# TensorE in emission order through a two-layer hybrid attention trunk

## The chip, the cores and the metric

The kernel runs on one core of a Trainium2 chip. The time is that of one execution on the device in microseconds (us). The profile comes from one execution that the hardware profiler recorded. Instructions are dispatched from one program per engine: TensorE (PE) does matmuls and transposes, VectorE (DVE) and ScalarE (ACT) elementwise work, GpSimd (POOL) little here, SyncE (SP) issues most transfers.

## The reference

Two layers of d_model 1024 over a sequence of 1024, float32. Each layer normalises its input, projects it once, and feeds two attention mixers whose outputs are gated, projected, merged and added to the residual:

```python
def hybrid_layer(x, c, ...):                       # cut to its steps
    h = rms_norm(x, norm_g) * (1 + scale(c)) + shift(c)
    parts = split(h @ w_in, IN_SIZES)              # all projections in one weight
    a = stick_breaking_attention(q, k, v)          # 8 heads of 64, blocks of 128 queries
    b = native_sparse_attention(q, kc, vc, ks, vs, kw, vw, gate_logits)
    a, b = a * silu(z_a), b * silu(z_b)
    y = sigmoid(m_a) * (a @ w_proj_a) + sigmoid(m_b) * (b @ w_proj_b)
    return x + gate(c) * (y @ w_out)

def stick_breaking_attention(q, k, v):             # per block of queries
    z = q @ k.T * scale
    between = reverse_cumsum(log_keep) - log_keep  # log_keep = log_sigmoid(-z), below the diagonal
    w = exp(log_sigmoid(z) + between)
    return w @ v
```

The sparse attention (NSA) has a branch over compressed keys, one over the eight best blocks of 64 keys, and one over a sliding window of 256.

## The kernel before

A layer goes through six parts: the norm (`norm_first` for layer 0; `norm_half`, called in the `output` of the layer before, for layer 1), `early` (the projections that NSA needs, compressed keys and values), `nsa`, `sb` (stick-breaking attention), what is left of the fill, and `output`.

**Projections.** Every operand is held as a high and a low float32r part, and a projection is three matmuls per chunk of 128 channels: L194 (high by high), L196 and L198 (high by low, low by high), in `mm3_gen`. A tile `proj` is 128x512 or 128x256, with eight chunks, so 24 matmuls.

**Fill.** `queue_projections` puts the stick-breaking projections (q, k, v) and then eight groups of gate projections (`t_group("m", ...)`) as generators into a list, `self.fill`. `run_jobs` goes through the attention jobs of `nsa` and `sb`: it merges the scores' steps of one job with the weights-times-values steps of the job before, emits one step, and calls `pump` with a share of the job's estimated us; `pump` emits projection matmuls from the list until that much is used up. `drain_fill` emits what is left. `tick` and `defer` emit vector steps when an estimated clock has come far enough, `flush` all of them at once.

**Order.** What the code emits goes to the tile framework's scheduler, which sets each engine's order and the semaphores. It puts instructions that it takes to be ready ahead of ones that wait. Code inside `tc.manual_schedule(engines={...})` keeps the emission's order on the engines named. Before, `norm_first` alone is inside one, for PE, DVE and ACT.

**Names in the rows.** `sc` are scores in PSUM (L996 compressed ones, L872, L873 the others, with L875 for the mask; `kk` stacked keys, `q` queries, `KCS` compressed keys). `E` and `C` are ScalarE's results from them (L1245, L1246 for stick-breaking), which VectorE finishes (L1249 the reversed product scan, L1250; L1115 in NSA). `tr` L885 are transposes of E, `wh` and `wl` their split parts (L137), `av` L904, L905 the products with V. `x` L430 is the scaled input of the second layer's norm, `tr` L436 its transposes, `acthi` and `actlo` the normalised input in two parts. `raw` and `w` are weights as loaded and as split. q and kk come by DMA from the DRAM tensor `QK`, where `early` and the fill put them.

Of the kernel before, what the change touches and what calls it, by code (L numbers as in the profile page):

```python
# [10 lines left out]
F32 = mybir.dt.float32  # L11
# [10 lines left out]
S = 1024  # L22
D = 1024
# [64 lines left out]
class Trunk:  # L88
# [214 lines left out]
    def run(self):  # L303
        tc, nc, I = self.tc, self.nc, self.I
        with tc.tile_pool(name="const", bufs=1) as cp, \
                tc.tile_pool(name="big", bufs=1) as self.big, \
                tc.tile_pool(name="wpool", bufs=1) as self.wpool, \
                tc.tile_pool(name="stage", bufs=2) as self.stage, \
                tc.tile_pool(name="lay", bufs=1) as self.lay, \
                tc.tile_pool(name="dram", bufs=1, space=DRAM) as self.dram, \  # L310
                tc.tile_pool(name="pproj", bufs=1, space=PSUM) as self.pproj, \
                tc.tile_pool(name="psc", bufs=1, space=PSUM) as self.psc, \
                tc.tile_pool(name="ptr", bufs=1, space=PSUM) as self.ptr, \
                tc.tile_pool(name="pav", bufs=1, space=PSUM) as self.pav:
            self.consts = self.tl(cp, [P, NMASK - 2 * P], F32, "consts")
            self.ident = self.tl(cp, [P, P], F32, "ident")
            self.sc = self.tl(cp, [P, KD], F32, "silu_c")
            self.ones = self.tl(cp, [P, P], F32, "ones")
            nc.vector.memset(self.ones, 1.0)
            self.identb = self.tl(cp, [P, P], BF16, "identb")  # L320
            self.mask = {m: self.tl(cp, [P, P], BF16, m) for m in ("m_strict", "m_causal")}
            self.mods = {}
            for l in range(self.depth):
                self.plan_layer(l)
            xsrc = I["x"]
            with tc.manual_schedule(engines={mybir.EngineType.PE, mybir.EngineType.DVE, mybir.EngineType.Activation}):
                act = self.norm_first()
            for l in range(self.depth):
                dst = self.O["out"] if l == self.depth - 1 else self.tl(self.dram, [S, D], F32, f"x{l + 1}")
                act = self.layer(l, act, xsrc, dst)  # L330
                xsrc = dst


    def vectors(self, pool, l):
# [1124 lines left out]
```

## Time and profile before

| | |
|---|---|
| time, median of three runs (lowest, highest) | 2232.81 us (2227.79, 2235.55) |
| profiled execution, its own time | 2227.61 us |
| its span, first to last instruction | 2225.8 us |
| mean granted clock of TensorE | 0.990 |
| busy share PE, DVE, ACT, POOL | 95%, 71%, 51%, 3% |
| HBM read, written | 206.28 MB, 83.89 MB |

An engine's busy time is the time in which it has an instruction under way. Matmuls overlap, so the sum of their single times is greater than the busy time. In the granted clock 1.00 is the full clock, 2.4 GHz, and 0.50 the lower one, 1.2 GHz. The layers take about half the span each: NSA runs in layer 0 from about 293 to 682 us, stick-breaking from there to about 1000, and the same in layer 1 about 1080 us later.

### The profile page before, as it was taken

How to read it: one execution, taken by the hardware profiler on the slowest of the kernel's cores; microseconds unless marked ns; L12 is line 12 of the kernel's file. 1: busy time of each engine (PE TensorE's matmuls, PEld its weight loads, DVE VectorE, ACT ScalarE, POOL GpSimd, SP SyncE). 2: the span in 40 equal slices, each digit the busy share in tenths (PEclk: the TensorE clock that was granted, in tenths of full speed). 3: DMA queues.
4: the chain of work that ended last, by engine and by line, in shares of the span. 5: the costliest groups of instructions: out<-in, count | busy, mean ns of one | idle time of the engine just before them, and what ended most of it. 6: DMA issues, size and time to landing. Idle time of an engine off the chain costs nothing.

```text
span 2225.8 us, 36846 instructions
## 1 busy us (share of the span) xinstructions
PE 2124.4 (95%) x13128; PEld 1833.5 (82%) x13128; DVE 1573.0 (71%) x3722; ACT 1129.9 (51%) x2489; POOL 73.0 (3%) x242
## 2 busy tenths in 40 slices
PE   4999999999999999999999998999999999999999
PEld 3898778988887777779889986889898877777899
DVE  5768558868765877886766852887788487787643
ACT  4433147656565655663433421665666465656410
POOL 2200000000000000010011000000000000001000
PEclk8999999999999999999999999999999999999999
DMA  7545852253116445275555355222522364534443
GB/s 287 113 136 189 251 154 81 91 152 94 64 48 159 128 130 129 81 245 177 164 151 161 107 192 141 90 90 82 146 92 68 97 151 113 146 98 166 148 124 104
DMA packets 254104, 297.05 MB, mean 133 GB/s; under 512 B 38888, under 2 KB 201568, under 8 KB 253920
## 3 DMA queue, kind: packets, MB, share of 16 engines
q1 hardware_dynamic: 213152, 250.65, 37.4%
q10 hardware_dynamic: 36224, 29.37, 5.1%
q0 software_dynamic: 4544, 14.68, 2.3%
q8 instruction: 103, 1.69, 0.3%
q14 instruction: 81, 0.66, 0.1%
HBM read 206.28 MB, written 83.89 MB: 130 GB/s over the span
## 4 chain that ended last, share of the span: by engine, by line
PE 66%; DVE 18%; DMA 7%; issue 4%; ACT 3%; POOL 1%; SPq 0%; ACTq 0%; DVEq 0%; POOLq 0%
PE proj L194 15%; PE proj L198 15%; PE proj L196 15%; PE tr L885 5%; DVE C L1249 4%; PE av L905 4%; PE av L904 3%; PE sc L872 3%; PE sc L873 3%; DVE wl L137 3%; DMA ada<-in_ada_w 2%; DVE E L1250 2%; DVE w L137 2%; DMA q<-QK 1%; DMA actlo<-AD 1%
## 5 line engine op out<-in xcount | busy, mean ns | idle before, releaser
L194 PE MATMUL proj<-acthi,w 128*128 128x512 f32 x1312 | 537.6, 410 | 3.0 <-ACT acthi L136 2.2
L196 PE MATMUL proj<-actlo,w 128*128 128x512 f32 x1312 | 538.0, 410 | 0.0
L198 PE MATMUL proj<-acthi,w 128*128 128x512 f32 x1312 | 537.2, 409 | 0.0
L136 ACT CAST w<-raw 128x512 fp32r<-128x512 f32 (+1 forms) x296 | 183.3, 623 | 227.3 <-PE proj L198 129.7
L194 PEld LDWEIGHTS proj<-acthi,w 128*128 128x128 f32 x1312 | 250.2, 191 | 43.6 <-ACT acthi L136 2.7
L137 DVE TENSOR_TENSOR wl<-tr,wh 128x512 fp32r<-128x512 f32 (+2 forms) x432 | 257.0, 611 | 40.7 <-ACT wh L136 38.3
L196 PEld LDWEIGHTS proj<-actlo,w 128*128 128x128 f32 x1312 | 250.0, 191 | 38.1 <-DVE actlo L137 0.8
L198 PEld LDWEIGHTS proj<-acthi,w 128*128 128x128 f32 x1312 | 249.6, 190 | 37.1 <-DVE w L137 0.2
L137 DVE TENSOR_TENSOR w<-raw,w 128x512 fp32r<-128x512 f32 (+1 forms) x296 | 202.5, 689 | 81.9 <-ACT w L136 80.6
L136 ACT CAST wh<-tr 128x512 fp32r<-128x512 f32 (+2 forms) x432 | 221.3, 527 | 76.4 <-PE tr L885 71.3
L194 PE MATMUL proj<-w,acthi 128*128 128x256 f32 (+1 forms) x768 | 221.5, 289 | 5.4 <-DVE s L137 2.4
L905 PE MATMUL av<-wl,V 128*128 128x256 f32 (+1 forms) x864 | 217.6, 285 | 7.6 <-DVE wl L137 7.4
L198 PE MATMUL proj<-w,actlo 128*128 128x256 f32 (+1 forms) x768 | 221.1, 288 | 0.0
L196 PE MATMUL proj<-w,acthi 128*128 128x256 f32 (+1 forms) x768 | 220.0, 286 | 0.0
L904 PE MATMUL av<-wh,V 128*128 128x256 f32 (+1 forms) x864 | 216.7, 271 | 1.2 <-DVE o L923 0.5
L1249 DVE TENSOR_TENSOR_SCAN C<-C 128x128 f32<-128x128 f32 (+7 forms) x128 | 172.7, 1350 | 55.0 <-ACT C L1245 54.5
L885 PE MATMUL tr<-ident,E 128*128 128x128 f32 x1152 | 187.4, 276 | 24.2 <-DVE E L1250 23.4
L885 PEld LDWEIGHTS tr<-ident,E 128*128 128x128 f32 x1152 | 139.1, 140 | 68.1 <-DVE E L1250 35.4
L905 PEld LDWEIGHTS av<-wl,V 128*128 128x128 f32 x864 | 162.7, 188 | 31.0 <-DVE wl L137 19.7
L872 PE MATMUL sc<-kk,q 128*128 128x512 f32 (+3 forms) x512 | 176.8, 346 | 8.8 <-DVE mx L1085 4.1
L873 PE MATMUL sc<-kk,q 128*128 128x512 f32 (+3 forms) x512 | 175.5, 343 | 0.0
L904 PEld LDWEIGHTS av<-wh,V 128*128 128x128 f32 x864 | 163.0, 189 | 13.7 <-ACT wh L136 3.6
(247 smaller groups left out, 3902.8 us busy)
## 6 DMA issues: line engine op xcount, KB each, us to landing
raw<-in_w_in SPq DMA_DIRECT2D x168, 256.0 KB, 3.0
ada<-in_ada_w SPq DMA_DIRECT2D x48, 512.0 KB, 5.1
kk<-QK SPq DMA_DIRECT2D x48, 512.0 KB, 8.6
q<-QK ACTq DMA_DIRECT2D x64, 256.0 KB, 4.2
QK<-s SPq DMA_DIRECT2D x32, 512.0 KB, 3.0
MD<-sz SPq DMA_DIRECT2D x64, 256.0 KB, 2.5
QK<-s SPq DMA_DIRECT2D x48, 256.0 KB, 3.9
VD<-s SPq DMA_DIRECT2D x48, 256.0 KB, 2.0
```

The lines of the kernel that those rows point to most:

```text
L136: nc.scalar.copy(hi, src)
L137: nc.vector.tensor_tensor(lo, src, hi.bitcast(F32), ALU.subtract)
L194: nc.tensor.matmul(ps, lh, rh, start=(x == 0), stop=False)
L196: nc.tensor.matmul(ps, lh, rl, start=False, stop=False)
L198: nc.tensor.matmul(ps, ll, rh, start=False, stop=(x == n - 1))
L872: nc.tensor.matmul(ps, q, k[:, 0, c0:c1], start=True, stop=False)
L873: nc.tensor.matmul(ps, q, k[:, 1, c0:c1], start=False, stop=not masks)
L885: nc.tensor.transpose(pt[:, x * P:x * P + P], b, self.ident)
L904: nc.tensor.matmul(ps[:, c:d], lhsT, hi[:, a:b], start=(first and x == 0), stop=False, skip_group_check=True)
L905: nc.tensor.matmul(ps[:, c:d], lhsT, lo[:, a:b], start=False, stop=(last and x == n - 1), skip_group_check=True)
L1249: nc.vector.tensor_tensor_scan(rev, rev, rev, 1.0, ALU.mult, ALU.bypass)
L1250: nc.vector.tensor_tensor(e[:, 0:nk], e[:, 0:nk], c[:, 1:nk + 1], ALU.mult)
```

## The change

The whole loop over the layers, with `norm_first`, is put into `manual_schedule` for PE. `norm_first` keeps its own for DVE and ACT, nested in it. Each line from L333 on stands one line further down in the kernel after (L872 is L873 there).

```diff
-            with tc.manual_schedule(engines={mybir.EngineType.PE, mybir.EngineType.DVE, mybir.EngineType.Activation}):
-                act = self.norm_first()
-            for l in range(self.depth):
-                dst = self.O["out"] if l == self.depth - 1 else self.tl(self.dram, [S, D], F32, f"x{l + 1}")
-                act = self.layer(l, act, xsrc, dst)
-                xsrc = dst
+            with tc.manual_schedule(engines={mybir.EngineType.PE}):
+                with tc.manual_schedule(engines={mybir.EngineType.DVE, mybir.EngineType.Activation}):
+                    act = self.norm_first()
+                for l in range(self.depth):
+                    dst = self.O["out"] if l == self.depth - 1 else self.tl(self.dram, [S, D], F32, f"x{l + 1}")
+                    act = self.layer(l, act, xsrc, dst)
+                    xsrc = dst
```

Three places of TensorE's program follow, as they stand before and after. The numbers in a tile's name tell one tile from another; the last of them differ by two between the kernels.

The start of layer 0's NSA stage before: the first compressed scores (`sc_482`) stand behind a run of fill, of which two tiles' last rows are shown.

```order
L196 MATMUL proj_530_3169<-actlo1_29_138,w_460_2836 128x512
L198 MATMUL proj_530_3169<-acthi1_28_137,w_460_2836 128x512
L194 MATMUL proj_530_3169<-acthi1_28_137,w_462_2841 128x512
L196 MATMUL proj_530_3169<-actlo1_29_138,w_462_2841 128x512
L996 MATMUL sc_482_3010<-KCS_126_595,q_481_3007 128x16 x4
L996 MATMUL sc_497_3058<-KCS_126_595,q_481_3007 128x32 x4
L198 MATMUL proj_530_3169<-acthi1_28_137,w_462_2841 128x512
```

The scores of this and the next step, `sc_497`, stand together, in the middle of a fill tile. The same place after, where `proj_473` to `proj_476` are the modulation's and gate's products of `early`:

```order
L412 MATMUL proj_473_2967<-acc2_381_2339,ones_4_87 128x512
L412 MATMUL proj_474_2970<-acc2_381_2339,ones_4_87 128x512
L374 MATMUL proj_475_2973<-ones_4_87,acc1_387_2349 128x1 x8
L374 MATMUL proj_476_2984<-ones_4_87,acc0_388_2350 128x1 x8
L997 MATMUL sc_482_3012<-KCS_126_597,q_481_3009 128x16 x4
L194 MATMUL proj_496_3053<-acthi0_26_137,w_458_2833 128x512
L196 MATMUL proj_496_3053<-actlo0_27_138,w_458_2833 128x512
L198 MATMUL proj_496_3053<-acthi0_26_137,w_458_2833 128x512
```

The scores `sc_482` moved ahead of the first fill tile, `proj_496`, and of all that stood before them up to `proj_530`.

The start of layer 0's stick-breaking stage before:

```order
L194 MATMUL proj_1754_8268<-acthi0_26_135,w_1594_7555 128x512
L196 MATMUL proj_1754_8268<-actlo0_27_136,w_1594_7555 128x512
L872 MATMUL sc_1715_8101<-kk_1710_8090,q_1712_8095 128x128
L873 MATMUL sc_1715_8101<-kk_1710_8090,q_1712_8095 128x128
L875 LDWEIGHTS identb_5_89
L875 MATMUL sc_1715_8101<-m_strict_6_90,identb_5_89 128x128
L872 MATMUL sc_1718_8118<-kk_1710_8090,q_1712_8095 128x256
```

Here too the scores of two steps stand together inside a fill tile. The same place after:

```order
L194 MATMUL proj_1707_8046<-acthi0_26_137,w_1596_7562 128x512
L873 MATMUL sc_1715_8103<-kk_1710_8092,q_1712_8097 128x128
L874 MATMUL sc_1715_8103<-kk_1710_8092,q_1712_8097 128x128
L876 LDWEIGHTS identb_5_89
L876 MATMUL sc_1715_8103<-m_strict_6_90,identb_5_89 128x128
L196 MATMUL proj_1707_8046<-actlo0_27_138,w_1596_7562 128x512
L198 MATMUL proj_1707_8046<-acthi0_26_137,w_1596_7562 128x512
L194 MATMUL proj_1707_8046<-acthi0_26_137,w_1598_7567 128x512
L196 MATMUL proj_1707_8046<-actlo0_27_138,w_1598_7567 128x512
L198 MATMUL proj_1707_8046<-acthi0_26_137,w_1598_7567 128x512
L194 MATMUL proj_1707_8046<-acthi0_26_137,w_1598_7567 128x512
L873 MATMUL sc_1718_8120<-kk_1710_8092,q_1712_8097 128x256
```

The first stick-breaking scores, `sc_1715`, stand ahead of what is left of `proj_1707` and of the tiles after it up to `proj_1754`, and fill stands between them and the next scores, `sc_1718`.

The layer boundary before, where `proj_2759` and `proj_2761` are layer 1's first projections:

```order
L198 MATMUL proj_2759_13230<-acthi0_2550_12056,w_2702_12958 128x512
L194 MATMUL proj_2761_13268<-acthi0_2550_12056,w_2696_12943 128x512
L196 MATMUL proj_2761_13268<-actlo0_2551_12057,w_2696_12943 128x512
L198 MATMUL proj_2761_13268<-acthi0_2550_12056,w_2696_12943 128x512
L436 MATMUL tr_2725_13115<-ident_2_85,x4_2634_12508 128x128
L436 MATMUL tr_2727_13124<-ident_2_85,x4_2634_12508 128x128
L436 MATMUL tr_2729_13133<-ident_2_85,x4_2634_12508 128x128
L194 MATMUL proj_2761_13268<-acthi0_2550_12056,w_2696_12943 128x512
```

The transposes come one at a time, as x becomes ready, with projections between them. The same place after:

```order
L198 MATMUL proj_2713_13058<-w_2682_12816,yl0_2553_12061 128x256
L437 MATMUL tr_2725_13117<-ident_2_85,x4_2634_12510 128x128 x4
L437 MATMUL tr_2727_13126<-ident_2_85,x4_2634_12510 128x128 x4
L437 MATMUL tr_2729_13135<-ident_2_85,x4_2634_12510 128x128 x4
L437 MATMUL tr_2731_13144<-ident_2_85,x4_2634_12510 128x128 x4
L437 MATMUL tr_2733_13153<-ident_2_85,x4_2634_12510 128x128 x4
L437 MATMUL tr_2735_13162<-ident_2_85,x4_2634_12510 128x128 x4
L437 MATMUL tr_2737_13171<-ident_2_85,x4_2634_12510 128x128 x4
L437 MATMUL tr_2739_13180<-ident_2_85,x4_2634_12510 128x128 x4
L194 MATMUL proj_2759_13232<-acthi0_2550_12058,w_2696_12945 128x512
```

All 32 transposes of the norm's second half moved ahead of the first projection of layer 1; before, they were spread among these projections.

## Rows read from the trace of the kernel before

**Rows 1.** The page: span, and busy time, share and instructions of each engine.

```profile
span 2225.8 us, 36846 instructions
PE 2124.4 (95%) x13128; PEld 1833.5 (82%) x13128; DVE 1573.0 (71%) x3722; ACT 1129.9 (51%) x2489; POOL 73.0 (3%) x242
```

**Rows 2.** The page: the chain that ended last, share of the span by engine.

```profile
PE 66%; DVE 18%; DMA 7%; issue 4%; ACT 3%; POOL 1%; SPq 0%; ACTq 0%; DVEq 0%; POOLq 0%
```

**Rows 3.** Windows: length, busy (count) of PE, PEld, DVE, ACT, POOL, PEclk, DMA, GB/s.

```profile
210.00:260.00 50.00, 50.00 (x216) 40.38 (x216) 30.45 (x33) 11.16 (x19) 0.00 (x0) 1.00 0.85 267
700.00:740.00 40.00, 35.99 (x212) 27.65 (x211) 36.97 (x50) 29.28 (x67) 1.19 (x12) 1.00 0.44 119
800.00:900.00 100.00, 94.41 (x541) 76.24 (x540) 79.30 (x108) 59.85 (x136) 2.38 (x24) 1.00 0.49 130
```

**Rows 4.** Windows around the starts of NSA and stick-breaking in both layers.

```profile
292.80:303.80 11.00, 10.85 (x39) 8.36 (x40) 0.61 (x3) 1.28 (x1) 0.00 (x0) 0.82 1.08 236
682.30:692.40 10.10, 10.10 (x44) 7.89 (x42) 0.00 (x0) 0.59 (x1) 0.00 (x0) 1.00 1.06 260
692.40:694.80 2.40, 0.14 (x2) 0.11 (x1) 0.00 (x0) 1.28 (x1) 0.00 (x0) 1.00 1.14 266
696.00:699.40 3.40, 3.40 (x10) 2.62 (x9) 1.32 (x3) 0.74 (x2) 0.20 (x2) 0.50 1.06 216
1373.60:1382.60 9.00, 9.00 (x39) 6.92 (x37) 1.59 (x4) 1.28 (x1) 0.00 (x0) 1.00 1.07 287
1382.60:1389.10 6.50, 0.04 (x1) 0.00 (x0) 0.00 (x0) 0.00 (x0) 0.00 (x0) 0.72 1.10 244
1389.20:1395.70 6.50, 6.50 (x21) 5.53 (x21) 2.77 (x14) 1.20 (x4) 0.00 (x0) 0.50 0.51 110
1770.90:1780.90 10.00, 10.00 (x45) 8.08 (x43) 0.00 (x0) 1.87 (x2) 0.00 (x0) 1.00 1.07 269
```

**Rows 5.** The chain that ended last, from 285 us: start, us, what.

```profile
290.03 13.65 DMA q<-QK
```

**Rows 6.** Timeline of PE: start, us, instruction, [idle before, releaser].

```profile
407.87 0.55 PE L885 MATMUL tr<-ident,E 128*128 128x128 f32 x3
694.73 0.30 PE L872 MATMUL sc<-kk,q 128*128 128x128 f32 x1 [2.26 <-DMA kk<-QK]
700.04 0.35 PE L872 MATMUL sc<-kk,q 128*128 128x384 f32 x1
794.38 0.38 PE L905 MATMUL av<-wl,V 128*128 128x256 f32 x1 [0.31 <-DVE wl L137]
1148.38 0.52 PE L436 MATMUL tr<-ident,x 128*128 128x128 f32 x3 [0.19 <-DVE x L430]
1169.88 0.36 PE L194 MATMUL proj<-w,acthi 128*128 128x256 f32 x1 [1.42 <-DVE s L137]
```

**Rows 7.** Timeline of ACT and DVE at two of these places.

```profile
695.42 0.27 ACT L1246 ACTIVATE E<-sc 128x128 f32<-128x128 f32 x1
1147.48 2.84 DVE L430 TENSOR_SCALAR x<-x,nri 128x1024 f32<-128x1024 f32 x4
```

**Rows 8.** Windows of tile proj alone: length, PE, PEld, DVE, ACT, PEclk, DMA, GB/s.

```profile
63.80:83.20 19.40, 5.60 (x37) 5.08 (x37) 0.84 (x2) 0.73 (x2) 1.00 0.26 62
349.50:353.50 4.00, 3.29 (x12) 2.08 (x12) 0.00 (x0) 0.00 (x0) 1.00 0.43 131
354.50:359.50 5.00, 3.81 (x13) 2.28 (x13) 0.68 (x1) 0.12 (x1) 1.00 0.31 107
405.60:407.90 2.30, 1.81 (x13) 1.60 (x12) 0.42 (x1) 0.37 (x1) 1.00 0.17 66
596.90:599.60 2.70, 1.92 (x6) 1.07 (x6) 0.00 (x0) 0.31 (x1) 1.00 0.25 97
1141.70:1158.60 16.90, 14.89 (x57) 9.83 (x56) 1.67 (x4) 1.48 (x4) 1.00 0.63 139
```

**Rows 9.** Waits of PE: waiting and releasing group, us in total, times, longest us.

```profile
PE tr L885 <- DVE E L1250: 23.4, 38, 1.1
```

## The prediction

> **What bounds the kernel now.** I read the page's busy times first. TensorE's matmuls cover 2124.4 of 2225.8 us [rows 1], so 101.4 us of idle is all that there is. The chain that ended last runs 66% through TensorE, 18% through VectorE and 7% through transfers [rows 2]. TensorE therefore sets most of the time, and what makes it idle is added to the end, unless later idle time takes the delayed work back.
>
> Then I read the stages. In the dense stretch from 210 us 216 matmuls take all of 50 us, 0.23 us each [rows 3]: no room. In the stick-breaking stage the engine is busy 94.4 of 100 us against VectorE's 79.3, and in that stage's opening 40 us VectorE leads, 37.0 against 36.0 [rows 3]. Attention is a string of short waits, and fill projections stand in them. Who puts them there is the question: the emission (`pump`, by its own estimate in us) or the scheduler, which moves matmuls on top of that. In the order listings the two kernels have the same instructions, and most of TensorE's program reads alike in both. They part in clusters: the half-1 chunks of the first norm, the start of each NSA stage, the start of each stick-breaking stage, the layer boundary, and some two dozen small places. At each of them the order before has projections ahead of a waiting attention step or transpose, and the order after has them behind it.
>
> So the method is this. At each cluster I count the projections that ran before the waiting instruction and no longer can. If the waiting instruction becomes ready when it did before, TensorE now stands idle for that time, and the projections run later, in stages that have no room. The loss is then about their busy time.
>
> **The change part by part.** All sums are made against the profiled execution's own time, 2227.61 us; the median of the three runs, 2232.81, is 5.2 above it, and I add that at the end.
>
> *T1, the first norm.* From 63.8 to 83.2 us 37 projection matmuls of 5.6 us [rows 8] run between the waits of the norm's chunks on VectorE. In order they come behind. Bounds 0 (the same chunks may come a little sooner where no projection is in their way) and 5.6; I take 4.
>
> *T2, the start of the NSA stage, twice.* The first compressed scores need q, and the chain shows its transfer from 290.03 for 13.65 us, so until 303.68 [rows 5]. TensorE was busy 10.85 of the 11.0 us before it, with 39 instructions, all but one of them fill [rows 4]. The order after has the scores first: about 11 us of idle, at full clock 9.0 us of work put off (layer 1 has the same 39 in 9.0 us [rows 4]). A second place follows 46 us later, where twelve and thirteen projections, 3.29 and 3.81 us, stand in two waits of the scores and transposes for VectorE [rows 8]. The low end is the first place alone, 9; the high end both, 9.0 + 7.1 = 16. I take 13, since the second place's wait may shrink when VectorE's steps are fed sooner. Twice: 26.
>
> *T3, the start of the stick-breaking stage, twice.* The same pattern with kk: 10.1 us filled with 44 instructions, then 2.26 us of idle until the scores at 694.73 [rows 4, 6]. In order TensorE waits through all of it. Layer 1 has 45 in 10.0 us [rows 4]. Here something comes back. The order before also holds the third score matmul until 700.04 [rows 6], although ScalarE had emptied its buffer at 695.42 + 0.27 = 695.69 [rows 7]: 4.35 us that the emission's order doesn't have. So 10.1 - 4.35 = 6 at the low end; 11 at the high one, with nothing back and the small places after it; I take 8. Twice: 16.
>
> *T4, the layer boundary, once.* The 32 transposes of norm half 1 are emitted ahead of layer 1's first projections. They need x, which VectorE scales at 1147.48 for 2.84 us [rows 7], the first of them being ready at 1148.38 [rows 6], and they then go at the pace of the modulation. 57 projection matmuls, 14.89 us in a window of 16.9, filled this [rows 8]. In order they follow. A wait of 1.42 us at 1169.88 for the projections' own successors [rows 6] can vanish: 14.89 - 1.42 = 13.5, and as half 0's chunks have a small place of the same kind I take 14. Low end 9 (the wait for x ends sooner, nothing else does), high end 17, the whole window.
>
> *T5, seven smaller waits of each NSA stage.* In the first, thirteen projections (1.81 us) stand ahead of transposes that become ready at 407.87, when VectorE has scaled E; in the last, six (1.92 us) [rows 6, 8]. The seven add up to 15.4 us of projections. Bounds: half of it, 8, if a wait is partly the wait for steps that fill itself delayed; 17 with the smallest places that I left out. I take 14. Twice: 28.
>
> *T6, the stick-breaking stage's small waits.* About ten places per layer have three projections, 0.7 us, moved from ahead of a waiting step to behind it, as ahead of the av matmul at 794.38 that still waited 0.31 us [rows 6]. Before, these waits were not all covered either: 38 waits for E cost 23.4 us [rows 9]. Twenty times 0.7 is 14, if nothing comes back. The next uncovered wait can take some of it back, most of it at the low end, 4. I take 10, nearer to nothing coming back, since the waits for E come at every step.
>
> *T7, the granted clock.* After the idle 2.26 us ahead of 694.73 the row from 696.0 shows a granted clock of 0.50 for 3.4 us, and after the 6.5 us ahead of 1389.1 one of 0.50 for 6.5 us [rows 4]; that is the lower level, 1.2 GHz. Half a stretch is lost: 1.7 and 3.3 us. The change makes idle stretches of such lengths at four places that had none (layer 0's NSA start, both stick-breaking starts' longer ones, the boundary): 4 x 2.5 = 10. Low end 0, if no new stretch follows. The high end is the first rival.
>
> Nothing is added to any engine's work: the listings of the other engines change only near these places, GpSimd's not at all, and the number of instructions and transfers is the same. That the fill is taken later lets its weight loads go out later too, which I cost at nothing: SP's queue holds them ahead of need, and the q and kk transfers may land a little sooner for it, which lies within the low ends of T2 and T3.
>
> Sum: 4 + 26 + 16 + 14 + 28 + 10 + 10 = **108 us**. 2227.6 + 108 + 5.2 = **2341**.
>
> **The rivals.**
>
> *Clock.* If each of the 18 in-order stalls of T2, T3 and T5 is followed by a stretch at the lower level, not four places, T7 is 18 x 1.7 to 3.3, or 31 to 59 us. The other terms sum to 98: 2227.6 + 98 + 31 + 5.2 = 2362, up to 2390. For it: the two stretches named. Against it: fill projections follow each short wait at once, and the small waits of the trace before, up to 1.1 us for E [rows 9], leave a clock of 1.00 in the row from 800 us [rows 3]. The page "TensorE: Matmul & The Clock Gate" of the Trainium skill describes in its section "HAM oscillation — how this bites in real kernels" a kernel whose matmuls wait for a transfer at every tile and fall back to the low clock at every tile. By that account this rival would be the forecast, about 2376; the two rows with 0.50 agree with it, the row from 800 us doesn't for its shorter waits.
>
> *Smaller loss.* The short waits of T5 and T6 could cost nothing: the attention steps no longer stand behind fill, VectorE and ScalarE get their inputs sooner, so that the waits shrink and the later idle time takes the fill back. Then T1 to T4 remain, 4 + 26 + 16 + 14 = 60: 2227.6 + 60 + 5.2 = 2293. For it: those 23.4 us of waits for E [rows 9] are idle time that delayed fill can use. Against it: a wait that was covered by 13 projections [rows 8] is now bare. The page "Perfetto Trace Analysis" of the Trainium skill says, in "Identifying the Most-Contended Engine", that matmul busy time is a poor measure of how near a kernel is to its bound. If the 95% overstates, this rival gains; in the dense stretch the trace speaks against it, with 216 matmuls back to back.
>
> *Faster.* VectorE's chain, not TensorE, could be what ends the attention stages; then fill in front of scores and transposes delays the chain, and emission order lifts that. Its place is the stick-breaking start, its price 4.35 us (695.69 to 700.04 [rows 6, 7]), twice: 2232.8 - 8.7 = 2224. It decides if the work put off finds room: the 101.4 us of idle [rows 1] would take all of it. For it: VectorE leads in the first 40 us of that stage. Against it: it is 15 us behind in the 100 us from 800 [rows 3], and T4's stage has projections to do whichever way it goes.
>
> *No effect.* The moved projections fall into other waits one for one, or the scheduler's order and the emission's come to the same at run time because every queue waits anyway: 2232, give or take 7. The listings show 39 matmuls changing sides of one wait, so I give it little.
>
> **How the numbers follow.** The forecast has 0.60, clock 0.17, smaller loss 0.14, faster 0.05, no effect 0.04. About 0.3% is what a measurement of this kernel can tell from no change. Three cases are slower by more: 0.91; within it lies no effect, 0.04; faster 0.05. The ends of the terms add up to 0 + 18 + 12 + 9 + 16 + 4 + 0 = 59 and 5.6 + 32 + 22 + 17 + 34 + 14 + 59 = 184 us, which will not all meet on one side. The range from 2290 to 2385 keeps nearly all of the forecast, most of the clock rival and half of the smaller loss, and leaves out the rest, about 2 in 10.
>
> **What would show it.** In the profile after, TensorE's waits should list q at about 11 us per layer, kk at about 12 in layer 0 and 10 in layer 1, and x at the boundary at about 6 us or more; the busy total should stay within some 20 us of 2124 and the idle time grow by about 90. T7 shows as new stretches of 0.50 behind these waits, the clock rival as such stretches all through the NSA stage. Smaller loss shows if the waits in T5's places are short. The prediction is wrong if the stages between the clusters become shorter than they were: that is delayed fill finding room, and the step that fails then is that the loss equals the busy time moved.

## The result

The changed kernel takes 2333.47 us (median of four runs, 2331.44 to 2342.53) where the kernel before takes 2232.53 us beside it: a ratio of 1.0464, 95% interval 1.0435 to 1.0493, slower by about 101 to 104 us. The forecast was 2341, the range 2290 to 2385.

The profiled execution took 2331.58 us. Its page answers to [rows 1]:

```profile
span 2329.8 us, 36825 instructions
PE 2133.9 (92%) x13128; PEld 1846.2 (79%) x13128; DVE 1584.8 (68%) x3722; ACT 1136.5 (49%) x2489; POOL 72.4 (3%) x242
```

The span grew by 104.0 us. TensorE's busy time grew by 9.5 us with the same 13128 matmuls, so its idle time grew from 101.4 to 195.9, by 94.5. That is the form which the prediction gave: about 90 us of idle, and a busy time within 20 us of the old one. The next view says what the idle time waits for. It is the list of TensorE's waits (what waits, what released it, us in total, times, longest):

```profile
PE sc L997 <- DMA q<-QK: 28.4, 2, 15.1
PE sc L873 <- DMA kk<-QK: 27.9, 4, 12.3
PE tr L886 <- DVE E L1251: 24.6, 28, 1.6
PE tr L886 <- DVE E L1116: 21.6, 26, 1.7
PE av L906 <- DVE wl L137: 17.3, 24, 1.1
PE tr L437 <- DVE x L431: 9.0, 7, 6.5
PE sc L873 <- DVE mx L1086: 5.0, 6, 1.6
```

The waits for q and kk were 6.7 and 2.3 us; they are now 28.4 and 27.9. E from L1116 (L1115 before) stood with no row of note; now it has 26 waits of 21.6 us. The waits of stick-breaking for E [rows 9] hardly grew, 23.4 to 24.6 us. The one for x, 6.5 us, is at the layer boundary.

The timeline shows the long ones at their places (start, length, instruction, idle before it and its releaser):

```profile
306.21 0.99 PE L997 MATMUL sc<-KCS,q 128*128 128x16 f32 x4 [13.27 <-DMA q<-QK]
424.77 0.33 PE L886 MATMUL tr<-ident,E 128*128 128x128 f32 x1 [1.10 <-DVE E L1116]
727.04 0.45 PE L873 MATMUL sc<-kk,q 128*128 128x128 f32 x1 [11.42 <-DMA kk<-QK]
1194.65 1.05 PE L437 MATMUL tr<-ident,x 128*128 128x128 f32 x2 [6.47 <-DVE x L431]
1447.12 0.99 PE L997 MATMUL sc<-KCS,q 128*128 128x16 f32 x4 [15.09 <-DMA q<-QK]
1872.35 0.47 PE L873 MATMUL sc<-kk,q 128*128 128x128 f32 x1 [12.29 <-DMA kk<-QK]
```

And the windows behind these waits have the lower clock (from:to, length, busy and count of PE, PEld, DVE, ACT, POOL, granted clock, DMA, GB/s):

```profile
306.20:309.80 3.60, 3.59 (x11) 3.02 (x12) 1.51 (x9) 0.23 (x1) 0.00 (x0) 0.50 1.03 196
727.00:733.40 6.40, 6.36 (x18) 5.23 (x19) 1.83 (x4) 1.69 (x5) 0.20 (x2) 0.50 1.06 211
1195.00:1201.00 6.00, 5.20 (x20) 3.58 (x19) 5.21 (x8) 2.19 (x3) 0.00 (x0) 0.50 0.12 27
1447.10:1453.60 6.50, 6.48 (x19) 5.50 (x20) 3.01 (x17) 0.49 (x2) 0.00 (x0) 0.50 0.72 150
1872.40:1876.90 4.50, 4.50 (x14) 3.73 (x15) 0.77 (x3) 0.91 (x4) 0.10 (x1) 0.50 1.05 216
```

**Where the time came from.** The order of the two kernels meets again between the clusters. At such a point I take the start of the same instruction in both traces, and how much its delay grew since the point before. Idle is span less busy time of TensorE between the points; the clock's cost is half of the busy time that lies at half clock. All in us.

| stretch | from, to in the trace before | delay grew | idle grew | clock cost grew |
|---|---|---|---|---|
| first norm, early | 0 to 291.9 | 0.5 | 3.1 | -1.3 |
| NSA start, layer 0 | to 365.1 | 17.3 | 17.9 | -0.4 |
| rest of NSA, layer 0 | to 650.6 | 15.4 | 10.9 | 1.7 |
| stick-breaking start, layer 0 | to 726.8 | 8.2 | 7.9 | 1.5 |
| rest of it, layer 0 | to 1032.7 | 3.4 | 4.9 | 0.0 |
| norm half 0 | to 1075.4 | 2.1 | 1.8 | 0.0 |
| layer boundary | to 1169.9 | 11.9 | 7.7 | 4.5 |
| early, layer 1 | to 1302.5 | -0.8 | 0.1 | 0.0 |
| NSA start, layer 1 | to 1453.7 | 13.2 | 13.2 | 0.0 |
| rest of NSA, layer 1 | to 1739.2 | 17.8 | 11.9 | 3.4 |
| stick-breaking start, layer 1 | to 1811.3 | 12.3 | 11.0 | 2.3 |
| rest of it and output, layer 1 | to 2126.2 | 2.7 | 4.0 | 0.1 |

The rows sum to 104.0, 94.4 of idle and 11.8 of clock. They don't add up in each row, since matmuls that overlap less also count as busy, and ones that overlap more count as less.

### The profile page after: what moved, and what is told of

It reads as the page before. It is cut to its first block, busy times and chain, and to the rows that moved or that the text cites. A ratio compares the mean times of both kernels' runs of the same rounds, so it can differ in the third digit from the quotient of the medians.

```text
span 2329.8 us, 36825 instructions
## 1 busy us (share of the span) xinstructions
PE 2133.9 (92%) x13128; PEld 1846.2 (79%) x13128; DVE 1584.8 (68%) x3722; ACT 1136.5 (49%) x2489; POOL 72.4 (3%) x242
## 4 chain that ended last, share of the span: by engine, by line
PE 67%; DVE 18%; DMA 6%; ACT 3%; issue 3%; SPq 1%; POOL 1%; ACTq 0%; DVEq 0%; POOLq 0%
PE proj L196 16%; PE proj L194 15%; PE proj L198 15%; PE tr L886 5%; DVE C L1250 4%; PE av L906 4%; PE av L905 3%; PE sc L873 3%; PE sc L874 3%; DVE E L1251 2%; DMA kk<-QK 2%; DVE wl L137 2%; DVE w L137 2%; DMA q<-QK 1%; DMA actlo<-AD 1%
## 5 line engine op out<-in xcount | busy, mean ns | idle before, releaser
L137 DVE TENSOR_TENSOR wl<-tr,wh 128x512 fp32r<-128x512 f32 (+2 forms) x432 | 260.2, 612 | 65.1 <-ACT wh L136 62.7
L886 PE MATMUL tr<-ident,E 128*128 128x128 f32 x1152 | 191.2, 278 | 47.1 <-DVE E L1251 24.6
L906 PE MATMUL av<-wl,V 128*128 128x256 f32 (+1 forms) x864 | 217.5, 284 | 17.6 <-DVE wl L137 17.3
L873 PE MATMUL sc<-kk,q 128*128 128x512 f32 (+3 forms) x512 | 174.8, 341 | 36.8 <-DMA kk<-QK 27.9
```

Source lines behind the costliest of these rows:

```text
L137: nc.vector.tensor_tensor(lo, src, hi.bitcast(F32), ALU.subtract)
L873: nc.tensor.matmul(ps, q, k[:, 0, c0:c1], start=True, stop=False)
L886: nc.tensor.transpose(pt[:, x * P:x * P + P], b, self.ident)
L906: nc.tensor.matmul(ps[:, c:d], lhsT, lo[:, a:b], start=False, stop=(last and x == n - 1), skip_group_check=True)
```

## Experiments

Ratios are to the kernel before in runs beside it on the same chip, with their 95% intervals. A statement on one place rests on one trace of each kernel.

### One stage at a time

Three kernels set only a part in emission order; the scheduler keeps the rest. In the traces TensorE's order differs from the kernel before at that part's clusters alone.

```diff
-        self.nsa(l)
+        with self.tc.manual_schedule(engines={mybir.EngineType.PE}):
+            self.nsa(l)
```

> The kernel before with TensorE in emission order in the two NSA stages alone. In the changed kernel the delay over the kernel before grew there by 17.3 + 15.4 us in layer 0 and 13.2 + 17.8 us in layer 1, 63.7 in all. If the loss is made at each place by itself: 2232.5 + 64 = 2296, from 2291 to 2301, with waits for q of about 13 and 15 us. If later stages give part back when they have not lost time themselves (smaller loss): below 2285.

```diff
-        self.sb(l)
-        self.drain_fill()
+        with self.tc.manual_schedule(engines={mybir.EngineType.PE}):
+            self.sb(l)
+            self.drain_fill()
```

> The kernel before with TensorE in emission order in the two stick-breaking stages alone. The delay grew there by 8.2 + 3.4 us in layer 0 and 12.3 + 2.7 us in layer 1, 26.6 in all: 2259, from 2255 to 2263, if each place loses by itself. If VectorE's chain bounds the stage and gains from the lifted hold of the third score matmul (faster rival): 2224 to 2232.

```diff
+            with tc.manual_schedule(engines={mybir.EngineType.PE}):
                 act = self.output(0, xsrc, x1)
                 self.head(1, act)                  # early and queue_projections
+            # likewise norm_first with head(0), and output(1); nsa and sb outside
```

> TensorE in emission order in the first norm, both layers' early projections and the outputs with the layer boundary; the scheduler orders the NSA and stick-breaking stages. In the changed kernel the delay grew there by 0.5 + 2.1 + 11.9 = 14.5 us: ratio 1.0065, from 1.005 to 1.008, if each place loses by itself. With the runs of the NSA stages alone and the stick-breaking stages alone it should sum to the whole change's 1.046. If the loss at the boundary came from the attention stages' delays before it: under 1.003.

Measured: NSA alone 1.0257 (1.0240 to 1.0274), 57 us; stick-breaking alone 1.0124 (1.0106 to 1.0142), 27 us; norms and boundary alone 1.0070 (1.0052 to 1.0088), 16 us. Together 1.0451 against the whole change's 1.0464. The waits of the first two, stage by stage, have nearly the rows of the whole change in them. TensorE's waits with NSA alone in emission order:

```profile
PE sc L996 <- DMA q<-QK: 29.3, 2, 15.4
PE tr L885 <- DVE E L1250: 23.0, 38, 1.1
PE tr L885 <- DVE E L1115: 21.6, 26, 1.7
```

and with stick-breaking alone:

```profile
PE tr L885 <- DVE E L1250: 24.6, 28, 1.6
PE sc L872 <- DMA kk<-QK: 20.3, 2, 10.4
PE av L905 <- DVE wl L137: 14.0, 16, 1.1
```

With NSA alone, E in NSA has its 21.6 us and E in stick-breaking (38 times, 23.0) stays as before; with stick-breaking alone it is the other way round. So the loss is made at each place by itself, and next to nothing is paid back by a later stage: 3.0 us at the start of layer 0's stick-breaking with NSA alone, in its one trace. That is the premise of the sum, and it speaks against the rivals "smaller loss" and "faster". The interval of NSA alone (54 to 61 us) lies a little under the 64 us that I wrote down; its trace has 62.7, of which 4.8 came ahead of the first score.

### What the low clock costs

The changed kernel with idle matmuls in the four waits for q and kk:

```diff
+    def spin(self, n):
+        ps = self.tl(self.pproj, [P, 512], F32, "proj", bufs=2)
+        hi = self.act[0][0]
+        for x in range(n):
+            self.nc.tensor.matmul(ps, hi[:, 0, 0:P], hi[:, 0, :], start=True, stop=True)
...
             load_q(0)
+            self.spin((54, 62)[l])
...                                          # and (46, 50)[l] in sb
```

> The changed kernel, with matmuls whose result nobody reads (128x512, 54 and 62 of them ahead of the NSA stages' first scores, 46 and 50 ahead of the stick-breaking ones), so that TensorE is busy through the four waits but does no useful work in them. If idle before the wait is what lowers the granted clock behind it: the rows of 0.50 behind the four waits go, 4.0 + 6.5 + 6.4 + 4.5 us of busy time at half clock cost half of that less, about 11 us, and the time is 2323, from 2319 to 2327; the rest of the loss there stays. If the low clock behind the waits has another cause: 2333. If the extra matmuls last past the landing of q and kk: above 2333.

Measured 1.0460 (1.0440 to 1.0481): as a whole not to be told from the changed kernel, and the 2323 us expected did not come (median 2331.19). At the places it did what was expected of an idle wait as cause. The windows behind the four waits:

```profile
306.00:309.80 3.80, 3.80 (x22) 3.24 (x22) 2.41 (x13) 0.32 (x2) 0.00 (x0) 1.00 0.77 148
727.00:733.40 6.40, 6.28 (x33) 5.06 (x34) 2.76 (x5) 2.88 (x9) 0.20 (x2) 1.00 1.04 215
1451.80:1458.00 6.20, 5.95 (x33) 4.90 (x33) 3.47 (x20) 0.98 (x4) 0.00 (x0) 1.00 0.70 144
1872.00:1876.90 4.90, 4.90 (x28) 3.97 (x27) 1.83 (x4) 1.99 (x7) 0.20 (x2) 1.00 1.07 212
```

The clock is 1.00 in all four where it was 0.50, with about twice the matmuls in the same time, and the stretches behind the first scores are 1.5, 2.9, 2.6 and 2.1 us shorter, some 9 together. But the trace is only 3.9 us shorter in all. Of layer 0's NSA start the 1.5 us are lost again within 77 us, where a new stretch at half clock stands; 3.2 us came in between the end of layer 0's stick-breaking and norm half 0, 1.6 in norm half 0 at half clock, and 2.6 in layer 1's early part. None of this stands at the spun waits. The matmuls did not last past the landing of q in layer 1 either, where TensorE still waits:

```profile
1451.78 0.47 PE L1004 MATMUL sc<-KCS,q 128*128 128x16 f32 x3 [1.26 <-DMA q<-QK]
```

The cost of the clock at the starts is shown in the trace, not in the time.

### Fill ahead of the starts, not given back

```diff
             load_q(0)
+            self.pump(14.0)
             jobs = [cmp_job(0)]
...
             load(0)
+            self.pump(12.0)
             jobs = []
```

> The changed kernel, with 14 us of fill emitted ahead of each NSA stage's first job and 12 us ahead of each stick-breaking stage's first, everything still in emission order. If the loss at the four starts is work that lost its place before the wait: the waits for q and kk (13.3, 15.1, 11.4, 12.3 us, together 52) shrink to under 2 us each, the stretches at half clock behind them go (about 11 us of cost), and the time is 2333.5 - 63 = 2271, from 2264 to 2282. If only the idle goes and the clock stays low: 2281 or more. If the fill used there is missed later in the stages: 2300 or more.

Measured 1.0587 (1.0569 to 1.0605), 25 to 27 us slower than the changed kernel: my expectation failed, and the third case written down held. The waits for q are gone, those for kk fell to 9.2 us. But the fill is a finite stock, which the jobs' estimates spread to the stage's end. In the listing of the changed kernel 16 av matmuls of layer 0 stand behind the last fill matmul, here 80. The window of the last 49 us of layer 0's stick-breaking, first all instructions, then the tile `proj` alone (length, PE, PEld, DVE, ACT, POOL, clock, DMA, GB/s; without POOL in the second):

```profile
965.00:1014.00 49.00, 33.86 (x179) 28.18 (x178) 42.85 (x55) 28.72 (x63) 5.10 (x16) 0.79 0.12 39
```

```profile
965.00:1014.00 49.00, 0.00 (x0) 0.00 (x0) 0.00 (x0) 0.00 (x0) 0.79 0.12 39
```

No projection is left; VectorE is busy 42.85 of 49 us and TensorE 33.86, at a granted clock of 0.79. The end of the same stage in the changed kernel, again first all and then `proj` alone, has 39.18 us of projections and the full clock:

```profile
940.00:999.00 59.00, 54.07 (x312) 43.81 (x311) 48.84 (x64) 39.55 (x86) 6.60 (x18) 1.00 0.33 110
940.00:999.00 59.00, 39.18 (x121) 20.20 (x120) 0.00 (x0) 2.96 (x5) 1.00 0.33 110
```

With fill ahead VectorE, not TensorE, is the busier engine at the stage's end, and I take its chain to bound it there. The page of the run with fill ahead says what the exchange came to:

```profile
PE 2164.9 (92%) x13128; PEld 1869.7 (79%) x13128; DVE 1591.4 (68%) x3722; ACT 1140.9 (48%) x2489; POOL 72.3 (3%) x242
```

Of its span of 2354.0 us TensorE is idle for 189.1, only 6.8 less than in the changed kernel, though 47 us of wait for q and kk are gone: the idle time has moved to other waits. The busy time grew by 31.0 us with the same matmuls. By the measure of the table above the low clock costs 53.3 us here and 27.9 in the changed kernel, and these 25 us are about what this run is slower by.

### Fill ahead, given back

The same with 9 and 10 us, about the scheduler's amounts, taken off the following jobs' fill: half of each share, or 9% of each.

```diff
+    def ahead(self, us):
+        self.pump(us)
+        self.owe = us
+
+    def share(self, us):              # in run_jobs instead of pump
+        r = min(self.owe, us / 2)     # second kernel: us * 0.09
+        self.owe -= r
+        self.pump(us - r)
...           # self.ahead(9.0) ahead of NSA's first job, self.ahead(10.0) of stick-breaking's
```

> The changed kernel with 9 us of fill emitted ahead of each NSA stage's first job and 10 us ahead of each stick-breaking stage's first, about what the scheduler pulled ahead before; the jobs that follow emit half their share of fill until this is given back, so that the stock at the stage's end is as it was. If work put ahead and given back soon is what the scheduler's order gained at the starts: the four waits (52 us) shrink by 9 + 9 + 10 + 10 = 38 us and some 5 us of half clock go with them: 100 us above the kernel before becomes 57 to 62, some 1.027 of it. If the idle only moves to the jobs that get half their fill, or to the stage's end as with fill that isn't given back: 1.043 or more.

> As the run with the fill ahead given back at half share (9 and 10 us ahead, ratio 1.0415), but given back at 9% of each job's share, over some 110 us of fill instead of 20. There the four waits shrank, and 7 us of idle came back in each NSA stage's next 40 us. If that idle came from the jobs with half their fill: it falls to about 3.5 us as in the changed kernel, and the time is 10 to 20 us below that run's, ratio 1.033 to 1.037. If the idle is only pushed on, to later jobs: 1.039 to 1.045.

Measured 1.0415 (1.0398 to 1.0432) and 1.0388 (1.0362 to 1.0413). The first is far from the 1.027 that was expected if the place before the wait were all. The second lies between its two cases, 1.033 to 1.037 and 1.039 to 1.045, and its interval reaches into both, so it doesn't decide between them. In both the waits for q and kk are mostly covered (9.4 and 10.3 us of 56.3 are left), so more than 45 us of wait are gone, but only some 11 and 17 us of time: TensorE's whole idle time fell by no more than 23.5 and 28.1 us, and its busy time grew by 11.7 and 10.5 with the same matmuls. The run with half given back is 7.8 us shorter than the changed kernel at each stick-breaking start, but 2.0 and 1.9 us longer at the NSA starts, behind their first scores. What is left of the waits with half given back:

```profile
PE sc L1007 <- DMA q<-QK: 5.3, 2, 5.1
PE sc L882 <- DMA kk<-QK: 4.1, 2, 2.6
```

For the first NSA stage the windows from the first score to the 25th score product tell why its start gains nothing. They are of the kernel before, the changed one, and the one that gives half back:

```profile
303.80:345.90 42.10, 41.67 (x254) 34.24 (x255) 36.64 (x149) 31.89 (x95) 0.04 (x1) 1.00 0.34 100
```

```profile
306.20:363.70 57.50, 53.96 (x312) 45.36 (x313) 44.52 (x167) 34.92 (x98) 0.16 (x1) 0.97 0.26 75
```

```profile
303.70:361.60 57.90, 47.13 (x269) 38.76 (x270) 42.84 (x166) 34.66 (x97) 0.16 (x1) 0.91 0.27 79
```

With the scheduler TensorE runs 254 matmuls there with 0.4 us of idle. With a like number, 269, in emission order it is idle for 10.8 us and part of the time at half clock. The amount of fill is about the same, 67 and 62 projection matmuls; the scheduler has it standing in the waits, the emission evenly between the steps. So the loss at the NSA start isn't the bare wait for q alone: what is pulled ahead of it is missing in the steps behind it, unless what is left there is put where they wait.

### Where a job's fill stands

```diff
-        self.tail = 0.15
+        self.tail = 0.35
```

> The changed kernel with 35% instead of 15% of each job's fill emitted at the job's end, ahead of the next job's steps, and so much less between the steps; the amount is the same. If where the fill stands decides, not how much there is: the waits of the transposes for E (21.6 us in NSA, 24.6 us in stick-breaking) shrink, by about a third, 15 us, and the waits between a job's own steps (wl, 17.3 us, and the row maxima, 7.8 us) grow; the time moves with the sum of both, somewhere from 2318 to 2345. If the E waits stay above 40 us: they are set by VectorE's own pace and no place of the fill covers them.

Measured 1.0538 (1.0519 to 1.0557), 14 to 17 us slower than the changed kernel, just above the span that I gave. The same amount of fill, at other places; TensorE's waits:

```profile
PE av L906 <- DVE wl L137: 31.0, 54, 1.1
PE tr L886 <- DVE E L1116: 22.9, 26, 1.6
PE tr L886 <- DVE E L1251: 15.9, 23, 1.1
```

Stick-breaking's E fell by 8.7 us, wl rose by 13.7, and NSA's E didn't fall as I had expected. The place of the fill matters, but this one number can't set it well. The waits aren't all of it: of the 15.6 us by which this trace is longer, 6.0 are idle time and 9.6 busy time with the same matmuls, and what made these longer isn't shown; the low clock costs 5.2 us less here.

### The boundary's projections first

The changed kernel with layer 1's first two tiles on half 0 emitted ahead of what is left of half 1's norm:

```diff
+            if not last:
+                w = self.take()
+                self.first = [[self.t_unit(w, u, 0, [nxt[0]]) for u in range(2)], None]
...                                          # early takes these two tiles instead of its own
             self.flush()
```

> The changed kernel with layer 1's first two projection tiles (48 matmuls of 128x512 on the first half of the tokens, 11 us) emitted ahead of what is left of the second half's norm, instead of behind its 32 transposes. If the boundary's loss is their place: 7.7 us of idle and 4.5 us at half clock mostly go, 9 to 12 us faster than the changed kernel, 2322 to 2325 where that has 2333. If the transposes' own pace (VectorE's scaling and modulation) bounds the boundary whatever stands ahead: the same as the changed kernel within 3 us.

Measured 1.0455 (1.0435 to 1.0475), in time not to be told from the changed kernel. In the trace the stretch from half 0's first transpose to layer 1's first score is 7.8 us shorter, a little less than expected. The waits for x fell from 9.0 to

```profile
PE tr L437 <- DVE x L431: 3.1, 7, 1.2
```

and no half clock is left at the boundary. So the place of those projections is most of the boundary's 11.9 us, as far as one trace can show. The part of that execution up to layer 0's first score was 4.3 us longer, with more of it at half clock, which hides it in that trace; why the median of four runs gains no more than some 2 us is open.

### More fill ahead under the scheduler

The kernel before has its own waits for q and kk, 6.5 and 2.3 us [rows 4, 6]. Two kernels put more fill ahead there and leave the order to the scheduler: 11, 15 (NSA, layers 0 and 1) and 12 us, given back at half share, and 8, 15 and 12 us, given back at a tenth. The edit is the one above, in the kernel before.

> The kernel before (scheduler on TensorE) with the same two pieces of code: 11 and 15 us of fill ahead of the NSA stages' first jobs, 12 us ahead of the stick-breaking ones', given back at half share. The kernel before still waited 6.5 and 2.3 us for q and kk, with half-clock stretches behind (3.3 and 1.7 us of cost), and held a score matmul for 4.4 and 2.8 us. If more fill ahead closes these: 10 to 18 us faster than the kernel before, 0.993. If the scheduler's order was already as good: 0.998 to 1.002. If giving back costs more than the waits: above 1.003.

> The kernel before, its scheduler on TensorE, with 8 us (layer 0) and 15 us (layer 1) of fill ahead of the NSA stages' first jobs and 12 us ahead of the stick-breaking ones', given back at a tenth of each job's share instead of half. With half (ratio 0.999) the starts gained 3.0, 8.1, 3.3 and 1.8 us in the trace, and the NSA stages behind gave 2.3 and 7.0 back. If the jobs with half their fill gave it back: some 8 to 12 us are kept, ratio 0.995 to 0.9965. If a stage always needs its stock: 0.998 to 1.001.

Measured 0.9990 (0.9978 to 1.0001) and 1.0022 (1.0013 to 1.0032). In the first no wait for q or kk is left and the rows of half clock there shrink, yet the time doesn't move beyond the measurement: in its trace what is left of the NSA stages behind the starts (365.1 to 650.6 and 1453.7 to 1739.2 in the trace before) is 4.0 and 2.0 us longer. The second is a little slower, above both of its cases; TensorE's waits for stick-breaking's E grew there from 23.4 [rows 9] to 33.8 us:

```profile
PE tr L894 <- DVE E L1261: 33.8, 48, 1.3
PE sc L1006 <- DMA q<-QK: 1.7, 1, 1.7
PE sc L881 <- DMA kk<-QK: 0.8, 1, 0.8
```

The stock that goes ahead is missing behind. No kernel here is shown to beat the one before.

## Why the prediction was right, step by step

| term | predicted | by the two traces |
|---|---|---|
| T1 first norm | 4 | 0.5 |
| T2 NSA starts | 26 | 17.3 + 13.2 = 30.5 |
| T3 stick-breaking starts | 16 | 8.2 + 12.3 = 20.5 |
| T4 boundary | 14 | 2.1 + 11.9 = 14.0 |
| T5 smaller NSA waits | 28 | 15.4 + 17.8 = 33.2 |
| T6 smaller stick-breaking waits | 10 | 3.4 + 2.7 = 6.1 |
| T7 clock | 10 | 11.8, within the rows above |

Less the 0.8 that layer 1's early part gave back, the right column without T7's line sums to 104.0, against 108. Without their share of the clock T2 to T5 are 30.9, 16.7, 9.5 and 28.1.

**The premise held.** TensorE is the bound, so an in-order wait adds its idle time to the end, and the projections that had filled it run later. The three part kernels show that the places add up and that hardly any gives back to another. This was the step on which all hung, and the one that the rivals denied.

**T2** was sized on 11 and 9 us of idle; the waits came out at 13.3 and 15.1, since q landed 2.4 us later in layer 0's span and in layer 1 the old idle of 6.5 us [rows 4] was in the same wait, which so grew by 8.6. The rest of each start, 4.8 and 4.7 us of idle, is in short waits behind the first scores.

**T3** counted on 4.35 us given back by the third score, no longer held. That step failed. The third score followed the first by 5.3 us before [rows 6] and by 7.1 after:

```profile
727.04 0.45 PE L873 MATMUL sc<-kk,q 128*128 128x128 f32 x1 [11.42 <-DMA kk<-QK]
...
730.30 0.41 PE L873 MATMUL sc<-kk,q 128*128 128x256 f32 x1
...
734.18 0.34 PE L873 MATMUL sc<-kk,q 128*128 128x384 f32 x1
```

Emission order has fill between them, at half clock. Layer 0 still came out at the 8 that I took, since 2.26 us of its wait of 11.42 had been idle before and it grew by 9.2 only; layer 1, which had no such idle, lost 12.3. With this the "faster" rival lost its price, too: the hold wasn't lifted but replaced.

**T4** was right in its sum, not in its parts: 9.5 of it idle, 4.5 clock, which I had booked under T7. The 14.89 us of projections that it was sized on showed as 9.5 of idle.

**T5** is right in size and half right in its working. In layer 0 six of the seven places have a bare wait now. The first is the 1.10 us at 424.77 above, the others are

```profile
488.31 0.33 PE L886 MATMUL tr<-ident,E 128*128 128x128 f32 x1 [1.66 <-DVE E L1116]
507.18 0.30 PE L873 MATMUL sc<-kk,q 128*128 128x128 f32 x1 [1.72 <-DMA kk<-QK]
537.12 0.33 PE L886 MATMUL tr<-ident,E 128*128 128x128 f32 x1 [1.31 <-DVE E L1116]
575.05 0.33 PE L886 MATMUL tr<-ident,E 128*128 128x128 f32 x1 [1.13 <-DVE E L1116]
629.94 0.33 PE L886 MATMUL tr<-ident,E 128*128 128x128 f32 x1 [1.01 <-DVE E L1116]
```

At the seventh, at 516.70 us in the trace before, there is none. Together they are 7.9 us, where 13.7 of the 15.4 us of projections had stood; in layer 1 the same six have 8.7. So these waits alone give the low end, 8, and not the projections' busy time, and why they are shorter isn't shown. The rest of the 15.4 that layer 0 lost there is 3.0 us of other short waits, 1.7 of clock and 2.8 of matmuls that overlap less, none of which T5 had counted.

**T6 and T1** were sized too high: there the next uncovered waits took fill back. In the first norm four waits of its chunks grew from 0.9 to 5.5 us, and ones of 0.83, 0.64 and 0.30 us behind them are gone. In layer 0's stick-breaking waits of 0.72, 0.55, 0.53, 0.32 and 0.30 us are gone, so the displaced matmuls found some room, 6.1 us lost of 14 moved.

**T7** counted layer 0's NSA start as a place that had no low clock before. That was misread: its row from 292.80 [rows 4] has a granted clock of 0.82, and there the clock's cost fell by 0.4 us. The stick-breaking starts and the boundary have 1.5, 2.3 and 4.5 of the 11.8; another 5.1 came in T5's stages, which weren't counted, and the first norm's part gave 1.3 back.

**How much of it was luck.** The sum is closer than its terms. Without the clock, T1, T4 and T6 were 10.7 us too high together and T2 was 4.9 too low, which partly cancels. T3's 16.7 and T5's 28.1 fit their 16 and 28 in size, but not by the working given, and T7's 11.8 for 10 lies partly at other places than the four that were counted.

**The rivals.** Clock: the low level came behind the long waits and at three of the short ones (508, 1631 and 1652 us in the trace after), not at all 18; 11.8 us, not 31 to 59. The Trainium skill's page "TensorE: Matmul & The Clock Gate", section "HAM oscillation — how this bites in real kernels", describes a fall at every wait of a kernel whose waits are about 3 to 5 us. The trace agrees with it for the waits of 6.5 us and more from the first NSA stage on, and the kernel with idle matmuls shows the idle as the cause at the four starts. Most waits here of 1 to 2.5 us have no such fall; they are shorter than the page's, so the prediction read more into it than it says when it took it for the rival's 18 stalls. Smaller loss: the stages of T5 lost 33.2 us, and T6's 6.1, where it had nothing.

## What to carry to other kernels

A kernel whose busiest engine is shown at 95% can owe that to the scheduler's order: before fixing an engine's order to the emission's, count at each of its waits the work that now stands ahead of it and can't any longer; that count, with the low clock behind long waits, was the loss here within 4 us in 104, with single terms off by up to 5 us or so either way. Work that fills gaps is a stock: moving it ahead of one wait takes it from another. The order that is fastest here has it standing in the waits themselves, which an even spread by estimated time doesn't do.

## What was not expected of the hardware

With the starts' waits filled by matmuls that nobody reads, the granted clock behind them is 1.00 at once, and yet the time of the whole hardly moves: other stretches of the same execution are longer, which isn't shown to follow from it. TensorE's busy time isn't fixed by its matmuls either: the same 13128 took 2124.4 us in the kernel before, 2133.9 in the changed one and 2164.9 with fill ahead and not given back, most of the last difference at half clock. Where the low clock falls otherwise also shifts between executions: at the same code, layer 0 up to its first score, 11.8 us of busy time lay at half clock in the changed kernel's trace and 19.5 in that of the kernel with the boundary's projections first, with 4.3 us between them. Differences of some 4 us in all can't be read from one trace; those at a place can.
